# An MLP norm without GpSimd beside it, sums of squares moved to the vector engine, and key marks added by TensorE

## The chip, the cores and the metric

The kernel runs on one core of a Trainium2 chip. A core has five engines with a queue each: TensorE (PE: matmuls, with PEld its weight loads), the vector engine (DVE), the scalar engine (ACT), GpSimd (POOL) and SyncE (SP), which issues the DMAs here. Data lies in SBUF; matmuls write to the eight banks of PSUM, which GpSimd can't read. The metric is the device time of one execution in microseconds, lower is better. Every engine works through its own queue in the order of the program and waits at an instruction until what it needs is there.

## The reference

Two transformer blocks follow each other on one sequence of 512 tokens with 1024 features, all in fp32. The first block is a hybrid mixer with a scan and an MLP, each behind a norm with a shift and a scale that come from a conditioning vector. The second puts 16 meta tokens in front and has a sparse attention layer A, a differential attention layer B and two convolutional feed-forward layers. The parts that the change touches:

```
# first block: after the mixer
h = rmsnorm(x, norm_mlp_w) * (1 + scale_f) + shift_f
x = x + gate_f * (square(relu(h @ w_up)) @ w_down)
x = rmsnorm(x, norm_final_w)                      # end of the first block
# second block, layer A: each query keeps the k_top keys of highest score
s     = einsum('bqhd,bsd->bqhs', qib, ki) * IDX_DIM ** -0.5
score = einsum('bqh,bqhs->bqs', wib, relu(s));  score = where(vis, score, NEG_INF)
_, idx = top_k(score, k_top)                      # k_top = 128
logits = einsum(q, k[idx]) * scale + bias[idx];  p = softmax(where(valid, logits, NEG_INF))
o      = einsum(p, v[idx])
```

## The kernel before

The activations lie with features on partitions: eight tiles of 128 features by 512 tokens (528 with the meta tokens). A fp32 product is made of three fp32r matmuls: a weight unit `ws` of 128 x 1024 is loaded by SP, ACT rounds it to a high half `wh`, and another engine subtracts to get the low half `wl` (`Weights.make`, by default on GpSimd); an activation is split in the same way into `hh` and `hl`. TensorE then adds high times high, high times low and low times high in a PSUM bank (`gemm`). Three raw units and four split units are held at a time. The order on each engine is the order in which the Python code issues instructions; nothing is rescheduled.

**MLP norm** (`tail1`). TensorE makes w_out one tile of 128 features after another. For each, `add` updates the residual `x` (DVE), squares it (ACT), adds the square to `acc` (DVE) and multiplies by the norm's gain into `xa` (DVE). The last two tiles (`ends`) are computed in two halves of 256 tokens, so that the first half can be normed while TensorE makes the second: `sums(0)` sums `acc` over the partitions and takes the inverse root, `rows(0)` spreads it over the partitions (`rb`, PSUM), and `norm` makes `xa * rb`, `hh` and `hl` of each tile. After `N0` tiles of the first half the last tile's second half is added, then the other tiles follow. Then w_up begins with F matrices at once, for the first half of the tokens and then the second: k from 0 to 2 for the first two matrices, then for the others, then k = 3, then the rest; `SUM1` and `ROW1` say at which k the second half's sums and rows stand. `self.W.make(self.W.used + n)` makes weight units ahead of their use.

**Entry to the second block** (`Entry`, `FirstNorm`). Two norms follow each other, the first block's final one and layer A's. Both come from sums of squares (`acc1`, `acc2`) that `Entry.add` collects tile by tile on GpSimd. Layer A's first product uses the tiles before the norm; `FirstNorm.one` makes the factors for each token at k = 3 of that product and `two` spreads them at k = 6. The residual tiles `hs` are multiplied by the first norm's factor later (`FirstNorm.first`, on GpSimd, in the values stage).

**Layer A** (`layer_a`). The values stage goes over the query blocks 4, 3, 2, 1 and 0 (`ORDER`; block b sees 128b + 16 keys): a value product (`tg`), its scaling by DVE into `v`, some scores (`lg` by TensorE, `relu` by ACT, weighted sum `score` by DVE) and one top-k step. Such a step (`choose`) finds the eight highest of each row and overwrites them; 16 make 128. A last step turns `score` into a mask: 0 where chosen, 1e30 where not. The logits are negated, so the softmax takes the least. The heads' q and k products (`hq`) are cut into steps that fill TensorE's time. The attention loop (`pipeline`) then runs over 32 units (block, head), with the stages of a unit spread over iterations: `m` at once, `l` and `s` two later, `d` (division) four, `t` (transposes `tp`) six, `o` and `w` (output `po`) eight later. `s_mask` first finishes the top-k of the block and lets GpSimd add mask and bias into `bm`; `s_soft` adds that to the logits in PSUM on DVE and takes the row's least; ACT makes the exponential. Top-k steps are spread between by credits (`choices`).

## Time and profile before

| | us |
|---|---|
| median of 3 runs | 2362.16 (2360.67 to 2363.61) |
| profiled execution, device time | 2363.21 |
| its span, first to last instruction | 2361.4 |
| TensorE busy | 2286.5 (97%) |
| DVE busy | 1296.8 (55%) |
| ACT busy | 982.4 (42%) |
| GpSimd busy | 1066.4 (45%) |
| MLP norm, end of w_out to the start of the MLP | about 640 to 678 |
| entry to layer A, values stage, attention loop | about 1018 to 1054, 1054 to 1094, 1094 to 1224 |

All rows are of one execution. A timeline gives the start from the span's beginning, the duration, the engine, the line of the kernel, the instruction with `out<-in` and the shape, and in brackets how long the engine had idled before and who ended it. Instructions of one kind that follow each other are merged, and the duration is then that of all. Matmuls are pipelined: the distance of two starts is what one costs, the duration is longer. Most of the helpers' operations bear the helper's line, so L260 is every matmul and L266 every low half. PEclk is the granted clock of TensorE: 1.0 is 2.4 GHz, 0.5 is 1.2 GHz.

### The profile page before, as it was taken

To read this page: it belongs to the slowest core of one execution; us is meant where nothing else is said; L and a number is where in the kernel's file an instruction comes from. 1 tells how busy PE (TensorE), PEld (TensorE's weight loads), DVE (VectorE), ACT (ScalarE), POOL (GpSimd) and SP (SyncE) were. 2 spreads that over 40 slices of the span, in tenths; PEclk is the share of its full clock that TensorE was granted. 3 is DMA by queue.
4 is the path that set the end of the run, shared out by engine and by line. 5 is a ranking of instruction groups with operands and counts; after the bars stand their busy time and mean duration, and the time that the engine had idled before them with its cause. 6 is when DMAs were issued, how large, how long until landed. Compare 5 with 4: busy or idle time off the path is not lost.

```text
span 2361.4 us, 36818 instructions
## 1 busy us (share of the span) xinstructions
PE 2286.5 (97%) x14560; PEld 2052.0 (87%) x14560; DVE 1296.8 (55%) x2492; ACT 982.4 (42%) x1814; POOL 1066.4 (45%) x608
## 2 busy tenths in 40 slices
PE   7999999999999999998999999999999989999999
PEld 5777787878888888888889999999998888989898
DVE  7767995566573022129974734435456656625443
ACT  3445543352243133344454423324466654424332
POOL 0434534456434434665533443434764443444433
PEclk9999999999999999999999999999999999999999
DMA  8324434525443223342102332323322122332322
GB/s 281 108 90 130 145 104 138 171 85 169 129 161 107 90 89 91 91 135 91 55 10 85 93 110 72 108 72 90 95 73 73 50 64 63 90 107 81 109 79 90
DMA packets 95980, 240.68 MB, mean 102 GB/s; under 512 B 10560, under 2 KB 26048, under 8 KB 95808
## 3 DMA queue, kind: packets, MB, share of 16 engines
q1 hardware_dynamic: 95808, 238.32, 33.0%
q8 instruction: 115, 1.88, 0.3%
q14 instruction: 57, 0.47, 0.1%
HBM read 230.72 MB, written 4.33 MB: 100 GB/s over the span
## 4 chain that ended last, share of the span: by engine, by line
PE 73%; DVE 14%; ACT 7%; issue 3%; DMA 2%; POOL 1%; SPq 0%; ACTq 0%; DVEq 0%; POOLq 0%
PE mm L260 54%; PE dn L260 9%; PE hq L260 2%; DVE cv L263 2%; PE tg L260 2%; ACT wh L210 1%; DVE xbc L263 1%; PE po L260 1%; ACT p L257 1%; PE lg L260 1%; DVE score L1476 1%; DMA ada<-in_w_ada_dram 1%; DVE p L263 1%; DVE pw L245 1%; DVE hd L245 1%
## 5 line engine op out<-in xcount | busy, mean ns | idle before, releaser
L266 POOL TENSOR_TENSOR wl<-ws,wh 128x1024 fp32r<-128x1024 f32 (+3 forms) x353 | 836.3, 2374 | 1084.8 <-ACT wh L210 1002.2
L260 PE MATMUL mm<-hh,wh 128*128 128x264 f32 (+3 forms) x2280 | 610.9, 322 | 10.5 <-ACT hh L257 7.6
L260 PE MATMUL mm<-hh,wl 128*128 128x264 f32 (+3 forms) x2280 | 605.6, 320 | 1.5 <-POOL wl L266 1.5
L260 PE MATMUL mm<-hl,wh 128*128 128x264 f32 (+3 forms) x2280 | 605.7, 320 | 1.4 <-DVE hl L263 0.7
L210 ACT CAST wh<-ws 128x1024 fp32r<-128x1024 f32 (+3 forms) x361 | 365.2, 1020 | 218.7 <-PE dn L260 83.7
L260 PEld LDWEIGHTS mm<-hh,wh 128*128 128x128 f32 x2280 | 381.7, 190 | 47.8 <-ACT hh L257 9.6
L260 PEld LDWEIGHTS mm<-hl,wh 128*128 128x128 f32 x2280 | 380.5, 189 | 38.9 <-DVE hl L263 5.3
L260 PEld LDWEIGHTS mm<-hh,wl 128*128 128x128 f32 x2280 | 381.3, 190 | 33.1 <-POOL wl L266 2.3
L263 DVE SCALAR_TENSOR_TENSOR cv<-u,vecs,cv 128x527 f32<-128x527 f32 (+3 forms) x176 | 185.9, 1056 | 87.6 <-ACT cv L257 84.5
L260 PE MATMUL dn<-ch,wl 128*128 128x264 f32 (+1 forms) x528 | 140.7, 321 | 0.0
L260 PE MATMUL dn<-ch,wh 128*128 128x264 f32 (+1 forms) x528 | 140.7, 321 | 0.0
L260 PE MATMUL dn<-cl,wh 128*128 128x264 f32 (+1 forms) x528 | 140.6, 320 | 0.0
L245 DVE TENSOR_TENSOR u<-mm,rb 128x264 f32<-128x264 f32 (+1 forms) x176 | 67.3, 424 | 108.2 <-PE mm L260 107.4
L257 ACT ACTIVATE cv<-u,vecs 128x528 f32<-128x528 f32 (+1 forms) x88 | 72.5, 824 | 115.2 <-DVE u L245 114.9
L260 PE MATMUL hq<-hh,wh 128*128 128x264 f32 x384 | 116.6, 304 | 1.6 <-ACT pt L1668 0.9
L260 PE MATMUL hq<-hh,wl 128*128 128x264 f32 x384 | 109.8, 286 | 2.7 <-POOL wl L266 2.7
L260 PE MATMUL hq<-hl,wh 128*128 128x264 f32 x384 | 110.1, 287 | 0.0
L263 DVE SCALAR_TENSOR_TENSOR junk<-ada,cs 128x512 bf16<-128x512 f32 x96 | 101.6, 1096 | 12.2 <-DMA ada<-in_w_ada_dram 12.0
L260 PE MATMUL mm<-ul,wh 128*128 128x512 f32 x256 | 100.9, 394 | 0.0
L260 PE MATMUL mm<-uh,wl 128*128 128x512 f32 x256 | 100.8, 394 | 0.0
L260 PE MATMUL mm<-uh,wh 128*128 128x512 f32 x256 | 100.7, 394 | 0.0
L260 PEld LDWEIGHTS dn<-ch,wl 128*128 128x128 f32 x528 | 87.6, 188 | 7.8 <-POOL wl L266 0.3
(368 smaller groups left out, 4177.3 us busy)
## 6 DMA issues: line engine op xcount, KB each, us to landing
ws<-in_w_up_dram SPq DMA_DIRECT2D x120, 512.0 KB, 3.6
ws<-in_w_in_dram SPq DMA_DIRECT2D x65, 512.0 KB, 3.6
ada<-in_w_ada_dram SPq DMA_DIRECT2D x96, 256.0 KB, 5.6
ws<-in_w_down_dram SPq DMA_DIRECT2D x32, 512.0 KB, 3.7
ws<-in_w_dn_dram SPq DMA_DIRECT2D x32, 512.0 KB, 3.5
E<-acs_d SPq DMA_DIRECT2D x32, 256.0 KB, 4.4
ws<-in_w_bs_dram SPq DMA_DIRECT2D x16, 512.0 KB, 3.7
ws<-in_w_ia_dram SPq DMA_DIRECT2D x15, 512.0 KB, 3.6
```

The lines of the kernel that those rows point to most:

```text
L210: k.nc.scalar.copy(hi[:, :n_], st[:, :n_])
L245: self.nc.vector.tensor_tensor(out, in0, in1, op=op)
L257: self.nc.scalar.activation(out, x, f, **k)
L260: self.nc.tensor.matmul(out, a, b, start=start, stop=stop)
L263: self.nc.vector.scalar_tensor_tensor(out, in0, scalar, in1, op0=op0, op1=op1, **k)
L266: (eng or self.nc.vector).tensor_tensor(out, x, hi.bitcast(F32), op=SUB)
L1476: nc.vector.match_replace(s, m8, s, GONE)
```

## The change

- In `tail1`, the low weight halves from the last w_out tiles to the fourth w_up matrix are made by DVE, at other places: two after the first halves of the end tiles (whose `add` now comes after both products), one after the second half of the sixth tile's product, one after the fourth normed tile. The gain `xa` is made by ACT. Three tiles of the first half are normed ahead of the last tile's second half (N0 = 3), and four w_up matrices are begun (F = 4; the third is in the bank `yd`).
- In `Entry.add`, the last tile's squares are added by DVE. The first norm's sums stand one k earlier, the rows one later.
- In layer A, the `v` columns are scaled straight from PSUM, and the invisible corner of `score` is set by DVE. The mask becomes an fp32r tile `sel`, which TensorE adds to the logits by a product with an identity `identr`; GpSimd's `bm` is gone, and DVE adds the bias itself where it added `bm`. The products of `hs` with the first norm's factor move from the values stage into every fourth iteration of the attention loop.

```diff
-N0, SUM1, ROW1, F = 2, 3, 6, 3
+N0, SUM1, ROW1, F = 3, 4, 6, 4
-META_A, OUT_A, EARLY_B = 9, 2, 3
+META_A, OUT_A, EARLY_B, FIRST_A = 9, 2, 3, 4
 # tail1
-            self.ts(xa[m][:, c], x, af[:, m:m + 1], None, MUL)
+            act(xa[m][:, c], x, scale=af[:, m:m + 1])
                 self.gemm("w_out", m, mix, [(P[m][:, half(f)], half(f))], hooks, hold=not f)
-                if not f or m == ends[0]:
+                if f and m == ends[0]:
+                    self.W.make(self.W.used + 3, nc.vector)
                     add(m, P[m][:, half(f)], half(f))
-            self.W.make(self.W.used + 2)
+            if not f:
+
+                self.W.make(self.W.used + 2, nc.vector)
+                for m in ends:
+                    add(m, P[m][:, half(f)], half(f))
         norm(0, range(N0))
-        self.W.make(self.W.used + 3)
         add(ends[1], P[ends[1]][:, half(1)], half(1))
-        norm(0, range(N0, KD))
+        norm(0, range(N0, N0 + 1))
+        self.W.make(self.W.used + 4, nc.vector)
+        norm(0, range(N0 + 1, KD))
-             for x in ("mm", "mm", "mm", "yd")[:F]]
+             for x in ("mm", "mm", "yd", "mm")[:F]]
-            first = [(k, m) for ms in ((0, 1), range(2, F)) for k in range(3) for m in ms]
-            rest = [(k, m) for k in range(4, KD) for m in range(F)]
+            first = [(k, m) for ms in (range(F - 1), (F - 1,)) for k in range(N0 + 1) for m in ms]
+            rest = [(k, m) for k in range(N0 + 1, KD) for m in range(F)]
-            for k, m in first + [(3, m) for m in range(F)] + rest:
+            for k, m in first + rest:
 # FirstNorm
+        def sums1(self):
+            self.p1 = self.k.col_sums(self.acc1, self.k.TOK4)
-            return {3: self.one, 6: self.two}
+            return {2: self.sums1, 3: self.one, 7: self.two}
-            for x in self.hs[3 * i:3 * i + 3]:
-                k.pol(x, x, self.rb1, MUL)
+            k.pol(self.hs[i], self.hs[i], self.rb1, MUL)
 # layer_a
-            self.ts(x, ps[:, :264], r[:, j:j + 1], None, MUL)
-            self.ts(x[:, 256:264], x[:, 256:264], 8 ** -0.5, None, MUL)
+            self.ts(x[:, 0:256], ps[:, 0:256], r[:, j:j + 1], None, MUL)
+            self.ts(x[:, 256:264], ps[:, 256:264], r[:, j:j + 1], 8 ** -0.5, MUL, MUL)
-            nc.gpsimd.memset(s[0:64, L - 64:L], NEG)
+            nc.vector.memset(s[0:64, L - 64:L], NEG)
+            def mark(s):
+
+                sel[b] = t(F32R, "sel", L)
+                self.ts(sel[b], s, -2e38, -NEG, ALU.is_gt, MUL)
-            topk.append((100, lambda: self.ts(s, s, -2e38, -NEG, ALU.is_gt, MUL), b))
+            topk.append((100, lambda: mark(s), b))
-            u["bm"] = t(F32, "bm", L)
-            self.pol(u["bm"], self.bias[h][:, T - L:], sel[b], ADD)
-            u["ps"] = self.logits(((done["q", h][:, q0:q0 + 128], done["k", h // 4]),), L)
+            u["ps"] = self.logits(((done["q", h][:, q0:q0 + 128], done["k", h // 4]), (self.identr, sel[b])), L)
-            self.soft(x, u["ps"], u["bm"], s, s[:, 3:4], s[:, 2:3])
+            self.soft(x, u["ps"], self.bias[h][:, T - L:], s, s[:, 3:4], s[:, 2:3])
+        def others(i):
+            if i % FIRST_A == FIRST_A - 1 and i // FIRST_A < KD:
+                norm.first(i // FIRST_A)
 # Entry.add
-        self.acc1 = k.add_square(self.acc1, x, k.nc.gpsimd)
+        eng = k.nc.gpsimd if m < KD - 1 else k.nc.vector
+        self.acc1 = k.add_square(self.acc1, x, eng)
-        self.acc2 = k.add_square(self.acc2, y, k.nc.gpsimd)
+        self.acc2 = k.add_square(self.acc2, y, eng)
```

What this moves stands in the order of the instructions. First DVE in the MLP norm, from the inverse root of the first half's sums on (`rtok`), before the change:

```order
L344 RECIPROCAL rtok<-rtok 128x2
L263 SCALAR_TENSOR_TENSOR x<-mm,gm,x 128x256
L245 TENSOR_TENSOR sq<-sq 128x256
L252 TENSOR_SCALAR xa<-x,af 128x256
L245 TENSOR_TENSOR xa<-xa,rb 128x256 x2
L263 SCALAR_TENSOR_TENSOR hl<-xa,mod,hh 128x256 x2
L263 SCALAR_TENSOR_TENSOR x<-mm,gm,x 128x256
L245 TENSOR_TENSOR sq<-sq 128x256
L252 TENSOR_SCALAR xa<-x,af 128x256
L245 TENSOR_TENSOR xa<-xa,rb 128x256 x2
L263 SCALAR_TENSOR_TENSOR hl<-xa,mod,hh 128x256
```

and the same place after it, from the instruction behind that inverse root on:

```order
L266 TENSOR_TENSOR wl<-ws,wh 128x1024
L263 SCALAR_TENSOR_TENSOR x<-mm,gm,x 128x256
L245 TENSOR_TENSOR sq<-sq 128x256
L245 TENSOR_TENSOR xa<-xa,rb 128x256 x2
L263 SCALAR_TENSOR_TENSOR hl<-xa,mod,hh 128x256
L245 TENSOR_TENSOR xa<-xa,rb 128x256
L263 SCALAR_TENSOR_TENSOR hl<-xa,mod,hh 128x256 x2
L263 SCALAR_TENSOR_TENSOR x<-mm,gm,x 128x256
L245 TENSOR_TENSOR sq<-sq 128x256
L245 TENSOR_TENSOR xa<-xa,rb 128x256
L263 SCALAR_TENSOR_TENSOR hl<-xa,mod,hh 128x256
L266 TENSOR_TENSOR wl<-ws,wh 128x1024
```

A low half of a weight now stands ahead of the sixth tile's second half and another behind the fourth normed tile (tile 3); the third normed tile (tile 2) has moved ahead of the last tile's sum, and the gains are gone.

GpSimd at the end of the values stage, before the change (`bias` is a head's bias table, `score` the scores, `bm` mask plus bias):

```order
L1448 MEMSET bias 64x64
L1450 COPY bias_7948<-bias 16x16
L1471 MEMSET score 64x64
L266 TENSOR_TENSOR wl<-ws,wh 128x1024 x3
L1471 MEMSET score 64x64 x2
L266 TENSOR_TENSOR wl<-ws,wh 128x1024 x4
L248 TENSOR_TENSOR bm<-bias,score 128x528 x2
```

and after it (`h` is a residual tile, `rb_9482` the first norm's factor):

```order
L1458 MEMSET bias 64x64
L1460 COPY bias_7974<-bias 16x16
L266 TENSOR_TENSOR wl<-ws,wh 128x1024 x9
L248 TENSOR_TENSOR h<-h,rb_9482 128x528
L266 TENSOR_TENSOR wl<-ws,wh 128x1024 x2
L248 TENSOR_TENSOR h<-h,rb_9482 128x528 x2
```

No memset of scores stands ahead of the low halves any more, and the residual's products stand between the loop's low halves.

TensorE where the last block's first logits stand (`lg`, 144 keys), before the change:

```order
L260 MATMUL lg<-hd 128x272
L1663 MATMUL tp<-ident,p 128x128 x2
L1665 MATMUL tp<-ident,p 128x128
L260 MATMUL po<-pt,v 128x128 x2
L260 MATMUL po<-pt_7952,v 128x128
L260 MATMUL lg<-hd 128x144
L1663 MATMUL tp<-ident,p 128x128 x2
L1665 MATMUL tp<-ident,p 128x128
```

and after it:

```order
L260 MATMUL lg<-hd 128x272
L260 MATMUL lg<-sel,identr 128x272
L1677 MATMUL tp<-ident,p 128x128 x2
L1679 MATMUL tp<-ident,p 128x128
L260 MATMUL po<-pt,v 128x128 x2
L260 MATMUL po<-pt_7978,v 128x128
L260 MATMUL lg<-hd 128x144
L260 MATMUL lg<-sel,identr 128x144
L1677 MATMUL tp<-ident,p 128x128 x2
L1679 MATMUL tp<-ident,p 128x128
```

Behind each head's logits stands the product with the marks, and transposes and outputs of older heads stand behind it.

## Rows read from the trace of the kernel before

**Rows 1.** The page: busy times, the chain by engine, ACT's high halves

```profile
PE 2286.5 (97%) x14560; PEld 2052.0 (87%) x14560; DVE 1296.8 (55%) x2492; ACT 982.4 (42%) x1814; POOL 1066.4 (45%) x608
...
PE 73%; DVE 14%; ACT 7%; issue 3%; DMA 2%; POOL 1%; SPq 0%; ACTq 0%; DVEq 0%; POOLq 0%
...
L210 ACT CAST wh<-ws 128x1024 fp32r<-128x1024 f32 (+3 forms) x361 | 365.2, 1020 | 218.7 <-PE dn L260 83.7
```

**Rows 2.** Waits of TensorE, 590 to 690 us: total, times, longest

```profile
PE mm L260 <- ACT hh L257: 4.6, 2, 3.1
```

**Rows 3.** Waits of TensorE, 960 to 1260 us

```profile
PE po L260 <- DVE sx L1633: 3.1, 1, 3.1
PE hq L260 <- POOL wl L266: 2.7, 1, 2.7
PE lamp L260 <- DVE v L252: 1.7, 1, 1.7
...
PE ssp L260 <- POOL sq L362: 0.5, 1, 0.5
```

**Rows 4.** Windows in the MLP norm: length, busy us (count) by engine, PEclk

```profile
657.70:663.00 5.30, 5.30 (x23) 5.06 (x24) 4.03 (x11) 2.65 (x6) 0.00 (x0) 0.50 0.21 83
663.00:665.80 2.80, 2.80 (x25) 2.80 (x24) 0.00 (x0) 0.00 (x0) 0.00 (x0) 0.98 0.00 0
```

**Rows 5.** Windows in layer A

```profile
1079.50:1094.00 14.50, 9.75 (x54) 9.12 (x55) 12.78 (x29) 2.93 (x6) 4.87 (x4) 0.76 0.52 171
...
1130.00:1157.00 27.00, 26.47 (x195) 25.34 (x193) 26.02 (x74) 11.97 (x22) 13.53 (x8) 1.00 0.23 74
```

**Rows 6.** Timeline of TensorE, MLP norm: start, us, instruction, count [idle before]

```profile
652.52 0.39 PE L260 MATMUL mm<-hh,wh 128*128 128x256 f32 x1 [1.48 <-ACT hh L257]
...
665.83 0.61 PE L260 MATMUL rb<-ident,rtok 128*128 128x128 f32 x4
```

**Rows 7.** Timeline of GpSimd, MLP norm

```profile
646.47 4.97 POOL L266 TENSOR_TENSOR wl<-ws,wh 128x1024 fp32r<-128x1024 f32 x2 [8.32 <-ACT wh L210]
653.88 2.36 POOL L266 TENSOR_TENSOR wl<-ws,wh 128x1024 fp32r<-128x1024 f32 x1 [2.44 <-ACT wh L210]
```

**Rows 8.** Timeline of DVE, MLP norm

```profile
649.12 2.47 DVE L252 TENSOR_SCALAR xa<-x,af 128x256 f32<-128x256 f32 x1
...
654.26 2.25 DVE L245 TENSOR_TENSOR sq<-sq 128x256 f32<-128x256 f32 x1 [0.48 <-ACT sq L257]
...
657.68 0.48 DVE L263 SCALAR_TENSOR_TENSOR hl<-xa,mod,hh 128x256 fp32r<-128x256 f32 x1 [0.24 <-ACT hh L257]
...
658.42 0.48 DVE L263 SCALAR_TENSOR_TENSOR hl<-xa,mod,hh 128x256 fp32r<-128x256 f32 x1
```

**Rows 9.** Low weight halves made by DVE: ns lowest, median, highest

```profile
L266 DVE TENSOR_TENSOR wl<-ws,wh x8: 1224/1226/1227, 18.0 to 57.9; 128x1024 fp32r<-128x1024 f32 x8
```

**Rows 10.** Groups of GpSimd, 1060 to 1225 us

```profile
L248 POOL TENSOR_TENSOR bm<-bias,score 128x528 f32<-128x528 f32 (+3 forms) x32 | 29.9, 964 | 18.3 <-DVE score L254 15.7 <-PE po L260 2.6
...
L248 POOL TENSOR_TENSOR h<-h,rb 128x528 f32<-128x528 f32 x8 | 10.4, 1319 | 0.0
```

**Rows 11.** Timeline of DVE, values stage

```profile
1072.73 5.29 DVE L252 TENSOR_SCALAR v<-v 128x8 f32<-128x8 f32 x1
...
1088.81 1.98 DVE L245 TENSOR_TENSOR kcol<-vecs 128x1 f32<-128x1 f32 x1
```

**Rows 12.** Timeline of GpSimd, end of the values stage

```profile
1085.97 0.14 POOL L1471 MEMSET score<- 64x64 f32 x1 [6.41 <-DVE score L263]
```

**Rows 13.** Timeline of TensorE, two score products that follow each other

```profile
1064.04 0.34 PE L260 MATMUL lg<-kx,qz 128*128 128x400 f32 x1
1064.22 0.34 PE L260 MATMUL lg<-kx,qx 128*128 128x400 f32 x1
```

**Rows 14.** Timeline of TensorE, the last block's first logits and the wait

```profile
1210.39 0.44 PE L260 MATMUL lg<-hd 128*128 128x144 f32 x2
...
1214.59 0.91 PE L260 MATMUL po<-pt,v 128*128 128x128 f32 x6 [3.05 <-DVE sx L1633]
```

More of the change, by code (lines that the diff above doesn't have):

```diff
@@ L1159, in one @@
             self.r = k.small.tile([128, 8], F32, name="rtok", tag="rtok")
-            p1, p2 = k.col_sums(self.acc1, k.TOK4), k.col_sums(self.acc2, COLS)
+            k.rsqrt(r1[:, 1:5], self.p1, D, 1e-5)
             k.nc.vector.memset(r1[:, 0:1], 1.0)
-            k.rsqrt(r1[:, 1:5], p1, D, 1e-5)
+            p2 = k.col_sums(self.acc2, COLS)
             k.dve(m[:, :5], p2, r1[:, :5], MUL)
@@ L1193, in block2 @@
             nc.vector.tensor_copy(self.sum_all[F32R], self.ones)
+            self.identr = c.tile([128, 128], F32R, name="identr")
+            nc.vector.tensor_copy(self.identr, self.ident)
             self.lam = c.tile([128, 4], F32, name="lam")
@@ L1451, in values @@
             x = vt[j] = t(F32, "v", 264)
-            self.ts(x, ps[:, :264], r[:, j:j + 1], None, MUL)
-            self.ts(x[:, 256:264], x[:, 256:264], 8 ** -0.5, None, MUL)
+            self.ts(x[:, 0:256], ps[:, 0:256], r[:, j:j + 1], None, MUL)
+            self.ts(x[:, 256:264], ps[:, 256:264], r[:, j:j + 1], 8 ** -0.5, MUL, MUL)
         def scores(b):
             q0, L = self.queries(b)
-            s = sel[b] = t(F32, "score", L)
+            s = t(F32, "score", L)
             for h in range(8):
@@ L1486, in layer_a @@
                 next(scored)
-            if i < 3:
-                norm.first(i)
             for _ in range(TOP_V[i]):
@@ L1550, in s_mask @@
         def s_mask(u):
-            b, h = u["b"], u["h"]
-            L = self.queries(b)[1]
-            while any(c == b for _, _, c in topk):
+            while any(c == u["b"] for _, _, c in topk):
                 topk.pop(0)[1]()
-            u["bm"] = t(F32, "bm", L)
-            self.pol(u["bm"], self.bias[h][:, T - L:], sel[b], ADD)
         def s_logits(u):
@@ L1602, in layer_a @@
               "o": (s_out, 2 + c), "s": (s_soft, 2), "w": (s_low, 2 + c)}
-        self.pipeline(U, S_, STAGES_A, more, lambda i: i >= META_A and meta and meta.pop(0)(), end)
+        def others(i):
+            if i % FIRST_A == FIRST_A - 1 and i // FIRST_A < KD:
+                norm.first(i // FIRST_A)
+            return i >= META_A and meta and meta.pop(0)()
+        self.pipeline(U, S_, STAGES_A, more, others, end)
         assert not meta and not topk
```

## The prediction

> **What bounds the kernel now.** The page first: TensorE is busy 97% of the span, and the chain that ended last runs 73% on TensorE and 14% on the vector engine (DVE) [rows 1]. Hardly any time can go where TensorE runs without a gap, so I asked who TensorE waits for in the stretches that the change touches. In the MLP norm it waits twice, 4.6 us in all, both times for the high halves that ACT makes [rows 2]. Around the attention of layer A, DVE, GpSimd and TensorE's own operands hold it up: 3.1 us at an output product, 2.7 at a head product waiting for GpSimd's low weight halves, 1.7 at the lambda product, 0.5 at the sums of squares [rows 3]. Then the windows, which show what a wait costs behind itself: after the MLP norm's second wait TensorE runs 5.3 us at a granted clock of 0.50, the 1.2 GHz level, with 23 matmuls, and 2.8 us later at 0.98 with 25 [rows 4]. From 1079.5 to 1094 it is busy 9.75 of 14.5 us at a clock of 0.76, with DVE busy 12.78; from 1130 to 1157 both are nearly full, 26.47 and 26.02 of 27 [rows 5]. So in layer A two engines bound the stage together, and DVE's time counts almost as much as TensorE's.
>
> **MLP norm.** TensorE ends w_out at about 651.0 (the first wait, 1.5 of the 4.6, ends at 652.52), and at 665.83 it makes the second half's row factors [rows 6]. Between the two stand 54 matmuls of w_up (six k, three matrices, three products) at 2.8/25 = 0.11 to 0.12 us and four short sums, 6.9 us; 14.8 passed, so 7.9 are lost. 4.6 are the waits; the other 3.3 are the low clock (5.3 us at half pace lose 2.65) and waits under half a microsecond.
>
> Why it waits: GpSimd makes low halves from 646.47 to 651.44 and from 653.88 to 656.24 [rows 7]. DVE's gain of 256 columns, begun at 649.12, ends at 651.59, and its sum of squares, begun at 654.26, at 656.51 [rows 8], each within 0.3 us of GpSimd. So 2.1 and 1.8 us of DVE go there. The change takes GpSimd out and gives DVE four low halves at 1.23 each [rows 9], 4.9 us for 3.9. As a plain exchange it would lose 1.0, the lower bound of this term; 7.9 is the upper. What decides is where the four fall. Two stand ahead of the first half's sums, where DVE waits for w_out: TensorE meets those sums about 0.3 late. One stands where the first hold-up was, so the first normed tile comes at 652.5 as before. The fourth comes only after tile 3. Tiles follow each other in 0.74 [rows 8], so tile 2, which now stands ahead of the last sum, is whole at about 654.2; TensorE, with three products in each of three matrices for k 0 to 2, is busy until 652.5 + 0.4 + 27 x 0.12 = 656.1. From that held sum to the end of the next tile's low half 3.9 passed [rows 8]; without the 1.8 and the gain (0.3, now ACT's), with 1.0 ahead for the tile and its square, tile 3 is whole at 657.0: 0.6 us of wait. Then ACT's high half (1.02 [rows 1]) and DVE's cast put the fourth matrix at 658.8, a further 0.9, and 48 matmuls are done at 660.1. The row factors' place (24 more and the sums) is 663.3, with 18 matmuls more than before, 2.2 us. Gain 665.8 - (663.3 - 2.2) = 4.7 at full clock. Waits of 1.5, 0.4, 0.6 and 0.9 remain, and the clock may fall behind them: I take 1.1 off, less than half of the 2.65 seen. **Term: 3.6 faster**, between 2.0 and 4.7, the bounds at its far ends as above.
>
> The row shows DVE waiting for GpSimd's end, not sharing with it. The Trainium skill (SBUF — State Buffer, "Who interferes with whom") says the same: the pair of ports is locked for a whole instruction, and whichever starts second waits. It also says that a DVE instruction with two SBUF inputs waits for a GpSimd one that reads SBUF, and this speaks against a part of the change below: by it GpSimd's low halves, started earlier in the values stage, would hold DVE there. Rival 3 is that outcome.
>
> **Entry to layer A.** The last tile's two sums of squares go to DVE; the sums' wait of 0.5 [rows 3] goes. DVE's low half of that tile comes two sums later, some 1.4 us, but its matmul is the last k of eight. The row factors move one k later, which the evacuation doesn't see. **Term: 0.4 faster**, between 0 and 0.5.
>
> **Values stage.** Eight GpSimd products, 10.4 us [rows 10], leave this stage. One eight-column scaling of DVE sits from 1072.73 for 5.29 us behind them [rows 11]; all but some 0.2 is hold-up: 5.1. The second scaling now reads PSUM. The constant's product at 1088.81 takes 1.98 behind a low half [rows 11]; that low half now comes earlier, because the score memset that kept GpSimd's queue 6.41 idle [rows 12] goes to DVE. So DVE comes to its first head evacuation 5.1 to 7.0 us sooner. TensorE can follow: the waits of 2.7 and 1.7 vanish, and what it can regain in that window is 4.75 idle plus about half of the low clock's time, 7 or more. It then waits for DVE. I take the lower value, 5.1, since the low halves have to fall somewhere beside DVE. **Term: 5.1 faster**, bounds 0 (all given back to the two low halves, 4.97 for a pair [rows 7]) and 7.0.
>
> **Attention loop.** GpSimd's 32 mask sums, 29.9 us, go; the 8 products, 10.4, come [rows 10]. What DVE gets back of these 19.5 us lies between 0 and, by the share of the values stage (5.1 of 10.4), 9.6. Most of DVE's time here is the top-k's, whose instructions have one input, and TensorE is as full as DVE; I take **1.2 faster**. Four memsets on DVE at GpSimd's 0.14 [rows 12] are **0.5 slower**. The marks are 40 more matmuls. In the marks' number format (fp32r) matmuls of 400 columns start 0.18 apart [rows 13]; the norm's 0.12 for 256 stands for 264 and 272 and bounds 144: 16 x 0.12 + 8 x 0.18 + 16 x 0.12 = 5.3 us. Block 4's first five heads (0.24 each) stand in the full stretch: **1.2 slower**. Blocks 3 and 2 (2.4) use up TensorE's lead, which today ends as the 3.05 wait at 1214.59 [rows 14], and cost nothing. Here the change adds a wait: a block's logits now need its mark, and behind them in TensorE's queue stand transposes and outputs of older heads. Before, the last block's first logits (1210.39) and three transposes ran ahead of the wait; now they come after it, about 0.6 net of the softmax that ended the wait. With seven marks of 0.12 behind it, where nothing waits any more: **1.4 slower**. Bounds of the three marks' parts: 0.8 (all hidden but the last) and 5.3 with the whole 3.05 again.
>
> **Sum.** 3.6 + 0.4 + 5.1 + 1.2 - 0.5 - 1.2 - 1.4 = 7.2 faster. The profiled execution took 2363.2 (span 2361.4 and 1.8 around it), so 2356.0 on that scale; it stands 1.05 above the median of the runs, 2362.2, so the median should be 2355.0.
>
> **Rivals.**
> 1. More comes back: no low clock (4.7), 0.5 at the entry, the full 7.0, 2.4 in the loop, marks hidden but 0.8, memsets 0.5. 13.3 faster, 2348.9. For it: DVE bounds the stage from 1079.5 on. Against: the low halves and the moved products still need the same memory.
> 2. The clock stays low behind the smaller waits: the norm gives 2.0, the values stage loses 1.5 to a new wait for the head evacuation and the low clock behind it, the loop gives nothing back: 2.0 + 0.4 + 3.6 - 3.1 = 2.9, 2359.3. For it: the clock fell behind waits of 1.7 and 2.7; against: the norm's own first wait, 1.5, has no low clock right behind it, and less waiting is left than now.
> 3. The two low halves, started earlier, hold DVE's score sums (two inputs in SBUF) as the eight products do now: the values stage gives 0.1, the sum 2.2, 2360.0. For it: DVE's sum was held that way in the norm [rows 7, 8]; against: most of what DVE does here is top-k, with one input. The Trainium skill's rule above (SBUF — State Buffer, "Who interferes with whom") gives this outcome, and the trace agrees with it in the norm.
> 4. Slower: the marks chain TensorE to the top-k at every block. The place is the first logits of blocks 3, 2 and 1; it decides once DVE's mark of block 2 comes after TensorE reaches those logits. Price: three waits of 3.05 for one (6.1), the 40 marks paid in full (5.3), two more stretches of low clock (5.3), memsets 0.5: 17.2 against gains of 9.1, 8.1 slower, 2370.3. Against: of the waits for DVE in this loop one alone is long today, the last block's [rows 3, 14].
>
> **Numbers.** Forecast 0.57 (its own range 2351.5 to 2358.5), rival 1 0.17, rival 2 0.11, rival 3 0.09, rival 4 0.06. About 0.2%, 4.7 us, is what a measurement of this kernel can tell from no change. Faster by more: 0.50 of the forecast's 0.57, all of rival 1, 0.04 of the others: 0.71. Slower: 0.05. Within: 0.24. The range 2348.0 to 2360.5 takes in rivals 2 and 3 and most of rival 1.
>
> **What would show it.** In the norm: one wait near 1.5 and no 3.1, DVE sums at 0.4, low halves of 1.23 on DVE, and from w_out's end to the first half's last k no stretch at 0.50. In the values stage: no scaling of 5 us, no lambda wait, no head product waiting for GpSimd. In the loop: mark matmuls 0.12 apart, one wait at the last block's logits of 3 us or less, DVE full. I am wrong if TensorE's low-clock stretches stay, if scores beside the early low halves take as long as the products did, or if logits wait for marks at blocks 2 and 3.

## The result and the profile after

The changed kernel took 2350.09 us (median of 4 runs, 2348.14 to 2352.29) beside 2362.89 for the kernel before: ratio 0.9947, 95% interval 0.9930 to 0.9965, 12.8 faster. A second set of 4 runs gave 2346.41 beside 2363.10: 0.9931, 0.9916 to 0.9945, 16.7 faster. The forecast was 7.2 faster (2355.0, range 2348.0 to 2360.5). The direction was right and the first median lies in the range; the second lies 1.6 below it, and the sum of the first rival, 13.3, is nearer than the forecast's own. Both traces of the changed kernel are of the lowest time of their set (2348.14 and 2345.34), those of the kernel before (2363.21 and 2361.25) lie above their medians; in the mean the spans of the traces differ by 15.4 us.

The page of the profiled execution: busy times, the granted clock in 40 slices and the chain by engine.

```profile
span 2346.4 us, 36875 instructions
PE 2280.1 (97%) x14624; PEld 2049.0 (87%) x14624; DVE 1292.0 (55%) x2493; ACT 987.6 (42%) x1824; POOL 1025.3 (44%) x566
PEclk9999999999999999999999999999999999999999
PE 71%; DVE 14%; ACT 7%; issue 3%; DMA 2%; POOL 1%; SPq 0%; DVEq 0%; ACTq 0%; POOLq 0%
```

The page says nearly nothing: the shares are those of [rows 1]. What changed is in the waits. TensorE's, in the MLP norm (590 to 700), who waits for whom, total, times, longest:

```profile
PE mm L260 <- ACT hh L257: 1.5, 2, 1.2
PE mm L260 <- DVE wl L266: 0.2, 1, 0.2
PE mm L260 <- DVE x L263: 0.2, 1, 0.2
```

And around layer A's attention (940 to 1260):

```profile
PE lg L260 <- DVE sel L254: 3.3, 1, 3.3
PE hs L260 <- ACT hsq L257: 2.1, 2, 1.3
PE hq L260 <- DVE hd L245: 1.2, 1, 1.2
PE mm L260 <- DVE x L263: 0.9, 1, 0.9
PE tg L260 <- POOL wl L266: 0.9, 1, 0.9
```

In the norm 4.6 us of waits have become 1.9 [rows 2], and the half-clock stretch behind them is gone: of all the runs here, the five traces with the old norm have 3.4 to 10.2 us at a clock of 0.50 there, the nine with the new one none. In layer A the 2.7 for GpSimd, the 1.7 of the lambda product and the 0.5 at the sums are gone, with 1.2 for DVE's head evacuation in their place; the 3.1 for the softmax at an output product has become 3.3 for the mark of the last block [rows 3]. The longest entry of the kernel before stands neither in these rows nor in the prediction, TensorE's wait for ACT's squares of the heads:

```profile
PE hs L260 <- ACT hsq L257: 5.2, 3, 3.1
```

It is 2.1 now; the 3.1 of it, late in the loop, has become 0.9.

The mean granted clock of the whole span says more than the waits (second trace of the kernel before, then two of the kernel after):

```profile
core 0: 2359.4 us, clock 0.992
```
```profile
core 0: 2346.4 us, clock 0.996
```
```profile
core 0: 2343.6 us, clock 0.997
```

1 minus the clock, times the span, is 18.9 us against 9.4 and 7.0. That bounds what the half-clock stretches cost, since TensorE waits in a part of them. So up to some 10 of the 15 us can have come back as clock and not as waits.

Where the time went, from the starts of the same matmuls on TensorE's timeline (two traces of each kernel):

| stretch | before | after | faster | forecast |
|---|---|---|---|---|
| start to w_out's end | 651.0, 652.4 | 653.4, 651.3 | -0.6 | 0 |
| MLP norm and w_up | 98.6, 98.8 | 93.3, 93.3 | 5.4 | 3.6 |
| w_down | 267.7, 267.7 | 266.7, 266.7 | 1.0 | 0 |
| entry, to the first value product | 34.0, 34.0 | 33.6, 35.1 | -0.4 | 0.4 |
| values, to the first head's sums | 43.5, 43.7 | 35.3, 35.3 | 8.3 | 5.1 |
| attention loop, to w_oa | 129.0, 128.7 | 133.1, 131.4 | -3.4 | -1.9 |
| w_oa and first up products | 144.6, 144.6 | 143.9, 143.8 | 0.7 | 0 |
| the rest, with layer B | 993.1, 989.6 | 987.3, 986.8 | 4.3 | 0 |

Ten short matmuls (`rows<-ident,r`, 1.05 us) moved from the values stage into the loop with the residual products, so values gained 7.2 and the loop lost 2.4 like for like. The four places of the forecast gave 9.9 us together; 6 came from code that the change does not touch.

The rows that answer to [rows 4] and [rows 6]: the whole stretch from w_out's end to the second half's row factors, its first w_up matmul and the row factors.

```profile
653.44:665.54 12.10, 10.14 (x76) 9.34 (x77) 8.68 (x21) 6.00 (x13) 0.00 (x0) 1.00 0.28 88
654.67 0.38 PE L260 MATMUL mm<-hh,wh 128*128 128x256 f32 x1 [1.23 <-ACT hh L257]
665.54 0.61 PE L260 MATMUL rb<-ident,rtok 128*128 128x128 f32 x4
651.21 1.23 DVE L266 TENSOR_TENSOR wl<-ws,wh 128x1024 fp32r<-128x1024 f32 x1 [1.01 <-ACT wh L210]
```

12.10 us where 14.80 passed before, with 18 matmuls more, no GpSimd and a clock of 1.00 throughout; the low half on DVE takes 1.23 as in [rows 9]. In the values stage, DVE's longest hold and GpSimd's instruction beside it, then two of DVE's in the loop:

```profile
1057.91 2.94 DVE L263 SCALAR_TENSOR_TENSOR score<-relu,v,score 128x528 f32<-128x528 f32 x1
1057.89 2.40 POOL L266 TENSOR_TENSOR wl<-ws,wh 128x1024 fp32r<-128x1024 f32 x1 [6.73 <-ACT wh L210]
1179.36 1.49 DVE L252 TENSOR_SCALAR p<-p,sx 128x400 f32<-128x400 f32 x1
1180.77 1.40 DVE L254 TENSOR_SCALAR sel<-score 128x272 fp32r<-128x272 f32 x1
```

A score sum alone takes 0.77; begun 0.02 us behind a low half it takes 2.94. This is what remains of [rows 11]: the 5.29 and the 1.98 are gone. The scaling and the mark from 1179 on stand beside five of the moved residual products in a row (1178.05 to 1184.61).

### The profile page after: what moved, and what is told of

The parts are those of the page before. It is cut to its first block, busy times and chain, and to the rows that moved or that the text cites. A ratio compares the mean times of both kernels' runs of the same rounds, so it can differ in the third digit from the quotient of the medians.

```text
span 2346.4 us, 36875 instructions
## 1 busy us (share of the span) xinstructions
PE 2280.1 (97%) x14624; PEld 2049.0 (87%) x14624; DVE 1292.0 (55%) x2493; ACT 987.6 (42%) x1824; POOL 1025.3 (44%) x566
## 4 chain that ended last, share of the span: by engine, by line
PE 71%; DVE 14%; ACT 7%; issue 3%; DMA 2%; POOL 1%; SPq 0%; DVEq 0%; ACTq 0%; POOLq 0%
PE mm L260 53%; PE dn L260 9%; PE hq L260 2%; DVE cv L263 2%; ACT wh L210 2%; DVE xbc L263 1%; PE tg L260 1%; POOL wl L266 1%; ACT p L257 1%; DVE score L263 1%; PE po L260 1%; PE yd L260 1%; DVE score L1486 1%; DVE p L263 1%; DMA ada<-in_w_ada_dram 1%
## 5 line engine op out<-in xcount | busy, mean ns | idle before, releaser
L266 POOL TENSOR_TENSOR wl<-ws,wh 128x1024 fp32r<-128x1024 f32 (+3 forms) x349 | 827.3, 2375 | 1133.0 <-ACT wh L210 996.8
L260 PE MATMUL mm<-hh,wl 128*128 128x264 f32 (+3 forms) x2272 | 599.2, 318 | 1.7 <-POOL wl L266 1.5
L263 DVE SCALAR_TENSOR_TENSOR junk<-ada,cs 128x512 bf16<-128x512 f32 x96 | 107.2, 1155 | 13.9 <-DMA ada<-in_w_ada_dram 13.7
```

Source lines behind the costliest of these rows:

```text
L260: self.nc.tensor.matmul(out, a, b, start=start, stop=stop)
L263: self.nc.vector.scalar_tensor_tensor(out, in0, scalar, in1, op0=op0, op1=op1, **k)
L266: (eng or self.nc.vector).tensor_tensor(out, x, hi.bitcast(F32), op=SUB)
```

## The experiments

Theory: the four terms of the forecast, with their sizes wrong. Rivals: the gain of the norm comes from its order and not from GpSimd's absence; GpSimd in the loop costs as much as in the values stage; a part of the gain has nothing to do with waits. Each kernel was timed beside the kernel before on the same chip; ratios are with their 95% intervals.

**before_again**: no edit.

> The kernel before once more, unchanged, for a second trace of it. In the one pair of traces 9.4 us of the 15.0 us between the spans lie in stretches that the change touches (norm 4.7, entry 0.4, values 7.0 faster, attention loop 2.7 slower); the other 5.6 lie in stretches whose instructions are the same in both. Theory A (chance of one execution): a second trace of the same kernel differs from the first by 2 to 4 us in such stretches, and the stream of 512-column matmuls between 700 and 740 us, 233.0 ns apart before and 231.1 after, comes out anywhere between the two. Theory B (a lasting side effect of the change on unchanged code): the second trace repeats the first within 1 us stretch by stretch, with 233 ns again in 650 to 900 and 122 ns for 264 columns in 1250 to 1600. Median 2362 to 2363 by both.

0.9998 (0.9988 to 1.0007). The stretches that the change touches repeat within 0.3 us, but the rest with layer B came out 3.4 shorter. So half of one comparison of layer B can be chance, and stage lengths are the sharper instrument: theory B for the streams (233.0 again), theory A for layer B.

**norm_only** (the hunks in `tail1` and the constants) and **attn_only** (the hunks in layer A; norm and entry as before).

> The MLP norm's part of the change alone, the rest as before. By the forecast's term the kernel is 3.6 us faster than before (2359.3), by the trace of the whole change 4.7 (2358.2), with no stretch at a granted clock of 0.50 between w_out's end and the first half's last k. If the faster stream behind it (231 instead of 233 ns for 512 columns) hangs on the norm's new order, 2 us more (2356.2) and 231 ns in 650 to 900; if not, 233 ns there.

> The parts in layer A's attention (eight residual products moved to the loop, value scalings, memsets on the vector engine, marks by TensorE); norm and entry as before. By the forecast's terms 3.2 us faster (5.1 + 1.2 - 0.5 - 1.2 - 1.4): 2359.7. By the one trace of the whole change 7.0 in the values stage less 2.7 in the loop: 4.3 faster, 2358.6. If the 122 to 121.4 ns of the 264-column stream in 1250 to 1600 hangs on this part, some 2 us more, 2356.5.

0.9983 (0.9974 to 0.9993) and 0.9990 (0.9981 to 0.9999): 4.0 and 2.4 faster; the medians, 2356.42 and 2358.41, lie next to the last figure of the first expectation and to the second of the other. Norm and w_up gave 5.3 to 5.5 and w_down 1.0, values 8.2 to 8.3, all as in the whole. The loop lost 5.3 with 6.8 us at half clock in it, where the whole loses 3.4. The times do not add up: 4.0, 2.4 and 0.4 for the entry are 6.8, beside 12.5 and 16.3 by the ratios of the whole. What is missing lies in the half-clock stretch of the entry, 1.5 us, which both parts have and neither trace of before has, in the loop, and in layer B (989.5 and 990.0 beside 987.3 and 986.8). The streams are at 231 with the new norm alone and at 233 without it.

**no_marks**: GpSimd adds mask and bias again.

```diff
-            u["ps"] = self.logits((..., (self.identr, sel[b])), L)
-            self.soft(x, u["ps"], self.bias[h][:, T - L:], ...)
+            self.pol(u["bm"], self.bias[h][:, T - L:], sel[b], ADD)
+            u["ps"] = self.logits((...,), L)
+            self.soft(x, u["ps"], u["bm"], ...)
```

> The changed kernel with the mask sums on GpSimd as before (32 products of bias and mask) and no marks on TensorE; the eight residual products stay in the loop. By the forecast's terms the loop then pays no marks (2.6) but has 29.9 us of GpSimd back, which costs it 1.8: 0.8 faster than the changed kernel, 2349.3. Rival (the marks are what makes the loop 2.7 slower): 3 to 5 faster than the changed kernel, 2345 to 2347. Rival (GpSimd beside the vector engine costs the loop half its busy time, as it did in the values stage, so the marks pay): slower than the changed kernel by 5 to 10, 2355 to 2360, with vector instructions of 1.5 to 3 us beside the mask sums.

0.9965 (0.9952 to 0.9978), 2351.37, 1.3 and 5.0 above the changed kernel's two medians; the loop took 134.2, 1.1 to 2.8 longer than with marks. The first two expectations have the wrong sign and the third is too large: by the loop the exchange pays, but little; the whole is not clear of the changed kernel's spread. What GpSimd costs DVE in the loop is read from the groups of two DVE forms there, mean ns behind the comma. In no_marks (mask sums and products), in the changed kernel (products alone) and in late_products below (neither):

```profile
L245 DVE TENSOR_TENSOR hd<-hd,hf 128x528 f32<-128x528 f32 x8 | 7.3, 909 | 1.6 <-ACT hf L257 1.6
L252 DVE TENSOR_SCALAR p<-p,sx 128x400 f32<-128x400 f32 x8 | 6.0, 745 | 0.3
L252 DVE TENSOR_SCALAR p<-p,sx 128x528 f32<-128x528 f32 x8 | 5.5, 694 | 0.3
```
```profile
L245 DVE TENSOR_TENSOR hd<-hd,hf 128x528 f32<-128x528 f32 x8 | 5.6, 700 | 1.1 <-ACT hf L257 1.1
L252 DVE TENSOR_SCALAR p<-p,sx 128x400 f32<-128x400 f32 x8 | 5.3, 664 | 0.3
L252 DVE TENSOR_SCALAR p<-p,sx 128x528 f32<-128x528 f32 x8 | 5.1, 637 | 0.3
```
```profile
L245 DVE TENSOR_TENSOR hd<-hd,hf 128x528 f32<-128x528 f32 x8 | 5.6, 700 | 1.0 <-ACT hf L257 1.0
L252 DVE TENSOR_SCALAR p<-p,sx 128x400 f32<-128x400 f32 x8 | 3.4, 431 | 0.3
L252 DVE TENSOR_SCALAR p<-p,sx 128x528 f32<-128x528 f32 x8 | 4.0, 496 | 0.3
```

Instructions with one input in SBUF (the scaling of `p`) are held as well. The prediction left that out in the loop, though the 5.29 of its own [rows 11] is one. Summed over DVE's instructions of the loop behind the last scores, the time beyond the quickest of the same form in these traces, where it is over 0.1 us, is 9.3 us in no_marks, 4.1 in the changed kernel (three scalings and the mark of 1.40), none in late_products and products_back, and 4.5 to 4.7 before. The Trainium skill ("SBUF — State Buffer", "Who interferes with whom") counts a tensor_scalar among the forms that can take the port pair shared with GpSimd; these rows agree.

**after_again** and **no_entry** (the changed kernel, and the same without the hunks of `Entry` and `FirstNorm.one`).

> The changed kernel once more, unchanged: a second trace, and its time beside the kernels of this set. Where its first trace and this one agree within 0.3 us stage by stage, the stage lengths are the kernel's own; layer B, whose instructions are the same as before, may come out 2 us longer or shorter by chance. Median 2349 to 2351.

> The changed kernel without the part at the entry (the last tile's sums of squares on GpSimd again, sums and row factors at their old places). By the forecast's term 0.4 slower than the changed kernel (2350.5), the wait of 0.5 for GpSimd's square back. Rival: that wait is followed by a stretch at half clock, as in the two traces of a part of the change alone, where the entry took 1.5 and 1.6 longer than before; then 1.9 to 2.4 slower (2352 to 2352.5).

0.9931 (0.9916 to 0.9945) and 0.9953 (0.9938 to 0.9967). The entry in the two traces of after, then in no_entry; the number behind the engines is the clock:

```profile
1013.37:1046.95 33.58, 32.59 (x268) 32.41 (x269) 7.98 (x24) 12.85 (x20) 26.53 (x28) 1.00 0.50 159
```
```profile
1011.15:1046.30 35.15, 34.14 (x269) 33.94 (x269) 7.98 (x24) 12.84 (x20) 26.53 (x28) 0.95 0.50 151
```
```profile
1014.30:1049.80 35.50, 34.97 (x279) 34.89 (x278) 7.91 (x23) 12.79 (x21) 29.61 (x30) 0.95 0.43 134
```

At a clock of 0.95 they differ by 0.35: the term of 0.4 is right. The median, 2352.24, lies where the rival put it, but the half-clock stretch comes with and without the wait for the square: in five of the seven traces with it and in three of the seven without it. So the wait is not needed for the stretch; whether it makes one likelier is open. The other 5 us between the medians of this set lie in the loop's clock and in layer B, where both have the same instructions. after_again itself missed its expectation: 2346.41 is under 2349, and entry and loop differ from the first trace by 1.5 and 1.7, the half-clock stretches; the other stages behind w_out's end agree within 0.1, layer B within 0.6.

**products_back**: the eight products in the values stage again (`norm.first(i)` for i < 3, three tiles each).

> The changed kernel with the eight residual products of GpSimd back in the values stage. The loop of the change lost 2.7 to 3.3 where the forecast had 1.9, and the values stage gained 7.0 where it had 5.1. By the forecast's terms the products cost the loop 0.6, and the whole is 4.5 slower than the changed kernel (2354.6). Rival (the products hold the vector engine in the loop nearly as they did in the values stage, 4 of their 10.4 us): values stage 7 longer, loop 4 shorter, 3 slower (2353).

0.9966 (0.9953 to 0.9979). Values 46.2, 10.9 longer, with two half-clock stretches; loop 125.7, 5.7 to 7.3 shorter. Without the short matmuls' 1.05 the products cost 9.8 in the values stage and 4.6 to 6.3 in the loop. The median, 2354.17, is next to the forecast's 2354.6, but no term is: both places move by more than either theory said and partly cancel, and beside the changed kernel of the same set it is 7.8 slower. The rival, which had 4 in the loop, was nearer there. One hold in the values stage shows why:

```profile
1066.48 7.42 DVE L263 SCALAR_TENSOR_TENSOR score<-relu,v,score 128x400 f32<-128x400 f32 x1
```

A sum of 0.63 stood until the end of five products that followed each other with only short copies between.

**before_pad**: one small matmul and its wait in TensorE's queue ahead of w_up's full-width matmuls.

```diff
+                    ...
+                    nc.vector.memset(pa, 0.0)
+                    nc.scalar.copy(pb, self.mod[:, 32:40])
+                    self.mm(self.sm("pad")[:8, :8], pa, pb)
```

> The kernel before with one small matmul (8 x 8, of two tiles made for it, never read) and the one wait instruction that comes with it put into TensorE's queue ahead of the full-width matmuls of w_up; nothing else is changed. In all traces so far the steady stream of 512-column matmuls repeats a pattern of 24 intervals, one pattern with a mean of 233.0 to 233.1 ns in the kernels with the old norm and another of 231.0 to 231.1 in those with the new. Theory A (the pattern is set by how many instructions stand ahead of the stream in TensorE's queue, which the new norm makes odd instead of even): 231 ns between 690 and 745, and the MLP some 1.7 us shorter than before; 2360 to 2361. Theory B (it comes from the norm's new order itself, what GpSimd and the vector engine do beside it): 233 ns, the time as before.

1.0063 (1.0046 to 1.0079), 15 slower, as a miss of the design: the memset stood behind the norm on DVE's queue.

```profile
PE pad L260 <- DVE pada L1069: 13.0, 1, 13.0
```

It still answers: the intervals behind it are 233.0 with the same 24 values, which moved with the tiles. Theory A falls.

**shift_tiles**: the kernel before with every later tile one buffer on.

```diff
+        pad = t(F32, "pad", S)
+        nc.vector.memset(pad[:, 0:1], 0.0)
         h = [(t(F32R, "hh", S), t(F32R, "hl", S)) for _ in range(KD)]
```

> The kernel before with one more tile of 528 columns taken from the rotating buffers ahead of the MLP norm (one column of it is set, nothing reads it), so that every later tile lies one buffer on; TensorE's instructions are the same, one by one. The small matmul in the stream moved the pattern of 24 intervals with the tiles and left its mean at 233.0, so it goes with the operands (k and product) and not with the place in the queue. Theory A (it is set by where the operand tiles lie, which differs between the kernels with the old and the new norm): another pattern, with a mean that differs from 233.1 ns by over 0.5, and other means of the 264-column streams too; the whole 0 to 3 us away from before on either side. Theory B (it goes with the order of the work, not with the addresses): 233.1 ns again, and the time as before.

0.9993 (0.9984 to 1.0002). The first and the last of 241 successive 512-column matmuls of w_up, in before_again, after and shift_tiles:

```profile
689.64 0.39 PE L260 MATMUL mm<-hh,wh 128*128 128x512 f32 x1
745.57 0.39 PE L260 MATMUL mm<-hh,wh 128*128 128x512 f32 x1
```
```profile
685.68 0.39 PE L260 MATMUL mm<-hh,wh 128*128 128x512 f32 x1
741.15 0.39 PE L260 MATMUL mm<-hh,wh 128*128 128x512 f32 x1
```
```profile
688.86 0.39 PE L260 MATMUL mm<-hh,wh 128*128 128x512 f32 x1
744.19 0.39 PE L260 MATMUL mm<-hh,wh 128*128 128x512 f32 x1
```

55.93, 55.47 and 55.33 us for 240: 233.05, 231.1 and 230.5 ns. TensorE's instructions are the same in the first and the third; the tiles lie elsewhere. w_down was 1.5 shorter too. Theory A holds.

**norm_pool**: the norm's low halves on GpSimd again, all else as changed.

```diff
-                    self.W.make(self.W.used + 3, nc.vector)
+                    self.W.make(self.W.used + 3)
 ...
```

The two other calls, for `used + 2` and `used + 4`, change in the same way.

> The changed kernel with the nine low halves of the MLP norm on GpSimd again (they stand where the change has them), the new order, the fourth matrix and ACT's gains kept. Theory A (the norm's gain comes from GpSimd no longer holding the vector engine's sums): instructions of 2 us and more on the vector engine between w_out's end and the last first-half tile, TensorE waits 2 to 4 us longer there and may fall to half clock: 3 to 5 slower than the changed kernel. Theory B (the gain comes from the fourth matrix, the third tile ahead and ACT's gains, that is from more work for TensorE while it waits): within 1.

0.9955 (0.9940 to 0.9970). TensorE's waits between 640 and 690, and two held instructions of DVE:

```profile
PE mm L260 <- ACT hh L257: 1.6, 2, 1.4
PE mm L260 <- POOL wl L266: 1.4, 1, 1.4
PE ssp L260 <- DVE sq L245: 0.3, 1, 0.3
```
```profile
649.35 2.39 DVE L245 TENSOR_TENSOR sq<-sq 128x256 f32<-128x256 f32 x1 [0.84 <-ACT sq L257]
658.13 2.22 DVE L263 SCALAR_TENSOR_TENSOR hl<-xa,mod,hh 128x256 fp32r<-128x256 f32 x1 [0.25 <-ACT hh L257]
```

DVE is held for 2.0 and 1.7 again, as before the change, yet the stretch is only 1.3 longer, at full clock. And the 1.3 is not the held DVE, which makes TensorE wait 0.3 at the sums: it is TensorE's wait of 1.4 for a low half itself, which GpSimd makes in 2.35 us and DVE in 1.23. Neither theory's number came; theory B is nearer. The time beyond 1.3 is in the loop's clock and layer B.

**late_products**: DVE makes each residual product ahead of the evacuation in w_oa.

```diff
-            k.pol(self.hs[i], self.hs[i], self.rb1, MUL)
+        def late(self, i):
+            self.k.dve(self.hs[i], self.hs[i], self.rb1, MUL)
 ...
         for m in range(KD):
+            if late:
+                late(m)
```

> The changed kernel with the eight residual products taken out of the attention loop and off GpSimd: the vector engine makes each right ahead of the evacuation of the same tile in w_oa, where it sits idle 2 to 5 us at a time. Theory A (what is left of the loop's loss is GpSimd holding the vector engine, which in the loop loses 4.95 us that way with the products and 1.9 without, by the trace with the products back): 3 to 4.7 faster than the changed kernel, 2342 to 2343.5, GpSimd in the loop with low halves alone. Theory B (the loop is bound by TensorE with its 40 marks and by the top-k itself): within 1 of the changed kernel. Theory C (the eight products of 0.7 delay the evacuations and the tiles' sums behind them): 1 to 3 slower.

2346.23 beside 2361.26, 0.9933 (0.9920 to 0.9945). The loop took 127.8, 3.7 shorter than in the trace of after that has no half clock there, and w_oa is 0.2 longer: theory A by the trace. The wait for the last mark fell to 1.8, because DVE comes to that mark sooner. DVE's four masks in before_again, after_again and late_products, with the ns of one (lowest, median, highest) and the starts of the first and the last:

```profile
L254 DVE TENSOR_SCALAR score<-score x4: 235/362/1407, 1124.8 to 1215.3; 128x528 f32<-128x528 f32 x1, 128x400 f32<-128x400 f32 x1, 128x272 f32<-128x272 f32 x1, 128x144 f32<-128x144 f32 x1
```
```profile
L254 DVE TENSOR_SCALAR sel<-score x4: 234/398/1400, 1110.9 to 1202.6; 128x528 fp32r<-128x528 f32 x1, 128x400 fp32r<-128x400 f32 x1, 128x272 fp32r<-128x272 f32 x1, 128x144 fp32r<-128x144 f32 x1
```
```profile
L254 DVE TENSOR_SCALAR sel<-score x4: 234/333/426, 1109.0 to 1197.0; 128x528 fp32r<-128x528 f32 x1, 128x400 fp32r<-128x400 f32 x1, 128x272 fp32r<-128x272 f32 x1, 128x144 fp32r<-128x144 f32 x1
```

From the first to the last pass 90.5, 91.7 and 88.0 us. From there to w_oa it is 9.9, 10.4 and 10.4. TensorE's wait for the last one:

```profile
PE lg L260 <- DVE sel L254: 1.8, 1, 1.8
```

The ratio is that of the changed kernel all the same, so the time does not show theory A: the median is 0.2 under the second one of the changed kernel, above the 2342 to 2343.5 expected. Its layer B took 988.7, 1.4 to 1.9 longer, and the rest is within the intervals.

**late_last_pool**: late_products, with the last block's masks added by GpSimd.

```diff
-                sel[b] = t(F32R, "sel", L)
+                sel[b] = t(F32R, "sel", L) if b > 1 else s
 ...
+            if b == 1:
+                self.pol(u["bias"], self.bias[h][:, T - L:], sel[b], ADD)
 ...
```

> The kernel with the late products (the vector engine makes the eight residual products in w_oa), and the last block's eight masks added by GpSimd as in the kernel before (sums of 144 columns, 0.49 each), so that its logits carry no mark and run ahead of the top-k; the other three blocks keep their marks. The forecast put the last block's marks at 1.4 (0.6 for the order, 0.8 for seven marks of 0.12). Theory A (the term is right): the wait of 1.8 at the last block's logits goes and one of 1 to 2 at an output product takes its place; the loop is 0.5 to 1.4 shorter than with the late products alone, 2344.8 to 2345.7. Theory B (the chain through GpSimd, mark to sum to softmax, is as long as the order that it saves): within 0.5 of the late products, with a wait near 3 as in the kernel before.

2344.79 beside 2363.10, 0.9926 (0.9913 to 0.9940): the lowest median, 18.3 below its own runs of the kernel before, but its interval overlaps that of the changed kernel, so it is not shown to beat it. The loop is 0.5 shorter than in late_products, on the edge between the two theories: DVE's first to last mask take 88.0 in both, and from there to w_oa it is 10.0 instead of 10.4. The wait is at an output product again:

```profile
1198.68 0.57 PE L260 MATMUL po<-pt,v 128*128 128x128 f32 x3 [1.92 <-DVE sx L1658]
```

## Why the prediction was right, and where its sizes were not

**MLP norm, 3.6.** The step was followed nearly to the tenth: from w_out's end to the row factors it expected 12.3 at full clock and 12.1 were measured, so 4.8 faster with the 18 extra matmuls. What was wrong is the 1.1 taken off for a clock that did not fall: waits of 1.2 and of a few tenths left it at 1.00. The cause was told too simply. DVE is held behind GpSimd, but norm_pool shows that low halves on DVE are worth 1.3 once three tiles are normed first, a fourth matrix fills TensorE and ACT makes the gains, and that most of the 1.3 is the shorter low half and not the end of the holds. The other 3.5 came with that order; what low halves on DVE would give in the old order was not run. w_up's stream of full-width matmuls is 0.6 more.

**Entry, 0.4.** 0.35 to 0.4 at the same clock.

**Values stage, 5.1.** The mis-sized term: 7.2, above its upper bound of 7.0. All named holds left, the waits of 2.7 and 1.7 with them, and the half-clock stretches behind those: 6.8 us in each of the six traces with the products in this stage, none in the eight without. The lower of the two bounds was taken because the two low halves must fall somewhere beside DVE; they did, but one score sum of 2.94 and one of 1.27 are all that they hold. In DVE's excess over usual times the stage has 2.8 where it had 10.3, which is the term. Rival 3's mechanism is in the trace [rows 7, 8] and in the 2.94, with 2.8 us of hold where it put 5.0, and the stage gained its 7.2 all the same.

**Attention loop, 1.9 slower.** 1.5 (no half clock) and 3.2 slower. The relief from GpSimd was too large: 1.2 expected, but the time that DVE is held fell only from 4.6 us to 4.1, by 0.5. The 10.4 us of products hold it nearly as long as the 29.9 us of mask sums did; five of them stand in a row beside scalings and a mark.

The marks were hidden in part. From start to start, without the long wait, the logits and their marks take about 24.2 us in TensorE's queue where the logits alone took 18.4: 5.7 for the marks (5.3 counted, of which three heads of block 4, 0.7, stand in no term). The loop paid less, because its end hangs on DVE: w_oa comes 9.9 to 10.4 us behind DVE's last mask in the three traces of the two kernels that have no half-clock stretch there, and TensorE waits 3.3 us for that mark, with time over. The marks filled another wait than the one named: the 3.1 for ACT's squares shrank to 0.9, while the 3.05 at the last block stayed, as 3.3, where the prediction looked for 3 or less. What the marks cost in all, with DVE's holds counted in full, is an estimate from three pairs of traces: 2.1 (before_again and after_again), 2.4 (after_again and no_marks) and 1.6 (before_again and products_back). The prediction had 2.6. Of that the last block, put at 1.4, measures 0.5 in late_last_pool, net of GpSimd's sums there; so some 1.5 is left for the others, where it had 1.2.

**What no term had: 6 us.** w_down and w_oa gave 1.7 (w_up's 0.6 stands in the norm's 5.4), and shift_tiles shows that moving tiles alone does this. The rest with layer B was 4.3 shorter in the mean, 2.6 against the shorter of the two traces of before. Its instructions are the same; both traces of after lie (987.3, 986.8) below all twelve others (988.7 to 993.1). Why is not settled, but much of it looks like chance of the clock: TensorE ran 6.8 us at half clock there in both traces of after, 17.1 and 10.2 in those of before. Where it ran 13.7, four variants of the changed kernel took 989.9 to 990.9 and two of the kernel before (shift_tiles, before_pad) 990.2 and 991.1, so at the same half-clock time no gain of the change is shown. The clock is not all of it: attn_only, with 6.8, took 990.0.

The 9.9 of the four places and the 1.7 of the streams make 11.6, beside the 12.8 of the first set. So the forecast was right in its direction and in the places of the gain, and too low in their sizes; that one median of the same kernel falls inside its range and the other outside is chance.

Rival 1 named full clock in the norm, 7.0 in the values stage and hidden marks. The first two came, the third in part, and its 2.4 of relief in the loop did not; its sum is close because of the 6 us that neither had. Rivals 2 and 4 fell: the clock rose, and the logits wait for a mark at the last block alone.

## What to carry to other kernels

Where two engines bound a stage, ask on which of them its end hangs before pricing work on the other: 5.3 us of marks on TensorE cost the loop about 2, since DVE's last mask ends it. Read every wait of the stretch, the longest first. When two engines hold each other up, the price of one on the other is set by what stands beside it: eight products of GpSimd cost 9.8 us beside score sums, 3.7 to 4.6 in the loop at full clock (by late_products and products_back), and 0.2 when an idle DVE made them. Compare stage lengths of two traces of each kernel before explaining a median: here over a third of the gain in the traces lay in code that nobody had touched, and the largest part of that in a stage where executions of one kernel differ by 3.4.

## What the runs showed of the hardware

- The interval of steady matmuls depends on where their operands lie: 233.05 ns for 512 columns in before_again and 230.5 in shift_tiles with the same instructions, 231.1 in after, in a fixed pattern of 24 values (225 to 241 ns) per output tile that repeats within 1 ns from one execution to the next. Which property of the addresses sets it stays open.
- A stretch at half clock comes and goes between executions of one kernel: the entry had one in the second trace of after (0.95 over 35.15 us) and none in the first (1.00 over 33.58); over all 14 traces it was there in eight.
- A DVE instruction with one SBUF input, the scaling of 400 columns of `p`, took 431 ns in the mean without GpSimd's sums and products (late_products), 664 with the products (after) and 745 with both (no_marks).
